# Conditioning work in a two-layer encoder trunk: row blocks requested a step ahead, sums placed later, half of the work moved to the second weight group

## The chip, the cores and the metric

The kernel runs on one core of a Trainium2 chip, as one launch. The metric is the device time of the launch in microseconds. The comparison between kernels is made with unprofiled runs; the views of the trace come from one profiled execution.

The core has a matrix engine (TensorE, in the profile PE, its weight loads PEld), a vector engine (VectorE, DVE), a scalar engine (ScalarE, ACT), GpSimd (POOL) and a queue that issues most of the DMA transfers (SyncE, SP). Each engine carries out its own list of instructions in order and waits on semaphores for the others.

## What is computed

The reference is a trunk of two layers on x of shape (1, 512, 1024) in f32. A layer has three sublayers: a half-step SwiGLU FFN, a mixer (a state-space scan, an attention and a short convolution side by side), and a second half-step FFN. Every sublayer is conditioned on one vector c:

```python
mod = (c_act @ ada_w[l] + ada_b[l]).reshape(b, N_SUB, 3, 1, D_MODEL)   # shift, scale, gate for each sublayer

h = modulate(x, mod[:, 0, 0], mod[:, 0, 1])            # x * (1 + scale) + shift
y = swiglu_ffn(h, ffn1_w_in[l], ffn1_w_out[l])
x = layer_norm(ALPHA * x + 0.5 * mod[:, 0, 2] * y, ln_g[l, 0], ln_b[l, 0])
```

`swiglu_ffn` is `(silu(gate) * up) @ w_out` with `gate, up` the halves of `h @ w_in`; the inner width is 2816. `ada_w` has the shape (2, 1024, 9216), 75 MB in f32, and is read once: c is one row, so each of its 18 column blocks of 1024 is a product of a vector with a 1024x1024 matrix. This part is the one that the change touches.

## The kernel before, in words

**Sublayers.** They are numbered s = 0 to 5; s = 0, 2, 3, 5 are FFNs, s = 1 and 4 are mixers. The activations lie in four token tiles of 128. Every large product is made of three f32r matmuls (`mm3`): both operands are split into a rounded high half and the remaining low half, and high x low, low x high and high x high are added in PSUM. Weights are loaded by SP into raw tiles (`ri` for w_in, `ro` for w_out; two buffers), ScalarE writes their high half (`hi`, `ho`), VectorE the low half (`li`, `lo`).

**An FFN.** `ffn` goes through 11 pairs `jp` of 256 inner columns, the first six as group 0, the other five as group 1. For each pair two column units (gate and up) are loaded and split, then come 96 matmuls into the tiles `pf`, then Silu, the product (`af`) and its split (`ah`, `al`). After each group `out_proj` multiplies what the group made by its rows of w_out (tiles `po`), in two halves of 512 output columns, and folds the result into x with the gate. In the last group's second half the token tiles are finished one after the other: fold, layer-norm statistics, norm; then PE transposes the tile (`ptr`), ScalarE applies scale and shift (`hf`) and rounds (`hh`), VectorE writes the low half (`hl`). The last token tile's transposes come only in the next sublayer, behind its first products (`last_tile`): an FFN's pair 0 takes token columns 0 to 255 first, and in their midst (`POS`) calls `last_tile`; then it takes columns 256 to 511, for which the last `hl` is needed.

**The conditioning work.** `ada_acc` makes one accumulator of 1024 columns: eight row blocks `ra` of 512 KB are requested on SP (L233; two buffers), and VectorE multiplies each by a column of c and adds it to `acc`, in two halves of 512. Then `acc_split` splits the accumulator (`gh` on ScalarE, `gl` on VectorE; `gl` takes one of the two buffers of the row blocks), and a sum over the partitions follows as two matmuls with ones for each half (`acc_sum`): into `pg` for a gate, to which the bias is then added, or into `pm` for a scale or shift, from which VectorE takes the diagonal and reduces it (`dg`, `sums`). `ada_gate(s)` makes the gate of a sublayer, `ada_ss(s)` its scale and shift, two accumulators one after the other.

**Where it stands in the program.** These are generators, and the FFN advances them by ticks: one tick behind the loads of each column unit (two for each pair) and one behind each row unit of `out_proj` (three for each half). A tick adds a number of credits (2.7 for s = 0 and 3, 1.3 for s = 2 and 5), and each yield costs one; a yield of `TICK` ends the tick and leaves the credit that is there. What is left is drained behind token tile 0 of the last half of `out_proj`. The first FFN of a layer makes the gates of s and s+1 and the scales and shifts of s+1 and s+2 (six accumulators), the second FFN the gate of s and the scale and shift of s+1 (three; one for s = 5).

**What sets the order.** The program's order is a priority. A planner that works ahead of time sorts each engine's instructions by it and by when, on its own estimates, an instruction is ready; the result is a fixed list for each engine. `after(ins, prev)` forces an order on one engine: the first accumulation of an accumulator stands behind the last `hl` that was written in the program before it (`ln_done`), and so do the splits of pair 1. Nearly all instructions of TensorE, VectorE and ScalarE go through one helper, so they carry its line, L52; the views tell them apart by tiles.

## Time and profile before

| | us |
|---|---|
| median of 3 runs | 1988.9 |
| the runs | 1988.61 to 1991.4 |
| profiled execution, its own time | 1988.45 |
| span of the trace in it | 1986.7 |
| TensorE busy in the span | 1937.8 (98%) |
| VectorE busy | 1206.4 (61%) |
| ScalarE busy | 705.8 (36%) |

In the lines shown below, a group or a timeline row names the engine, the operation, the tile it writes, `<-`, the tiles it reads, the shapes and a count. A timeline row begins with its start and its length in us, and a bracket tells how long the engine had stood idle before it and what ended that. A row of the waits reads: who waited, for whom, us in total, how often, the longest. Matmuls overlap, so TensorE's busy time is not its time at full rate.

### The profile page before, as it was taken

The numbers are of one execution on the slowest core, as the hardware profiler recorded it, in microseconds if no ns is written. First come the engines' busy times: TensorE is split into PE (matmuls) and PEld (weight loads), VectorE is DVE, ScalarE is ACT, GpSimd is POOL, SyncE is SP. The second block draws the span as 40 slices with busy tenths as digits, with TensorE's granted clock in tenths as the row PEclk, the third lists the DMA queues.
The fourth block names the chain that finished last, engine by engine and source line by source line (L and its number), as shares of the span: only waits on it lengthen the run. The fifth ranks groups of instructions, "written<-read, shape, count | busy, mean of one in ns | idle before, by whom it ended". The sixth has DMA issues, their size and how long they took to land.

```text
span 1986.7 us, 23052 instructions
## 1 busy us (share of the span) xinstructions
PE 1937.8 (98%) x9230; PEld 1616.3 (81%) x9230; DVE 1206.4 (61%) x1804; ACT 705.8 (36%) x1126; POOL 97.8 (5%) x126
## 2 busy tenths in 40 slices
PE   5999999999999999999999999999999999999998
PEld 4787888888878888888888788788888788888887
DVE  8886753477867655643478757436786676333336
ACT  3432222264575332132253222323546643222220
POOL 0100000012100000000000000000140000000000
PEclk9999999999999999999999999999999999999999
DMA  9675542143222544432256656322322243223321
GB/s 329 213 256 193 186 163 96 54 128 106 85 75 82 173 140 167 138 128 83 98 170 201 222 165 227 102 89 65 119 84 96 75 141 129 92 91 121 106 85 43
DMA packets 176730, 263.95 MB, mean 133 GB/s; under 512 B 9806, under 2 KB 124628, under 8 KB 176624
## 3 DMA queue, kind: packets, MB, share of 16 engines
q1 hardware_dynamic: 174000, 254.98, 38.7%
q0 software_dynamic: 2624, 7.52, 1.3%
q8 instruction: 72, 1.18, 0.2%
q14 instruction: 34, 0.28, 0.0%
HBM read 260.37 MB, written 2.10 MB: 132 GB/s over the span
## 4 chain that ended last, share of the span: by engine, by line
PE 81%; DVE 8%; DMA 6%; ACT 3%; issue 1%; POOL 0%; SPq 0%; POOLq 0%; DVEq 0%; ACTq 0%
PE pf L52 39%; PE po L52 26%; DMA ra<-in_ada_w_dram 5%; DVE acc L52 2%; PE pz L52 2%; PE pjm4x L52 1%; PE pjm1x L52 1%; ACT hf L52 1%; DVE li L52 1%; DVE af L52 1%; PE py L52 1%; DVE x L52 1%; PE pfo L52 1%; PE pjm1c L52 1%; PE pjm1k L52 1%
## 5 line engine op out<-in xcount | busy, mean ns | idle before, releaser
L52 PE MATMUL pf<-hl,hi 128*128 128x512 f32 (+1 forms) x1504 | 567.1, 377 | 7.5 <-DVE hl L52 7.5
L52 PE MATMUL pf<-hh,li 128*128 128x512 f32 (+1 forms) x1504 | 567.6, 377 | 1.5 <-DVE li L52 1.2
L52 PE MATMUL pf<-hh,hi 128*128 128x512 f32 (+1 forms) x1504 | 566.4, 377 | 0.0
L52 PEld LDWEIGHTS pf<-hl,hi 128*128 128x128 f32 x1504 | 284.7, 189 | 59.9 <-DVE hl L52 8.8
L52 PEld LDWEIGHTS pf<-hh,li 128*128 128x128 f32 x1504 | 284.7, 189 | 53.0 <-DVE li L52 1.7
L52 PEld LDWEIGHTS pf<-hh,hi 128*128 128x128 f32 x1504 | 284.6, 189 | 50.6
L52 DVE TENSOR_TENSOR li<-ri,hi 128x1024 fp32r<-128x1024 f32 x176 | 214.0, 1221 | 181.6 <-ACT hi L52 181.3
L52 ACT ACTIVATE hi<-ri 128x1024 fp32r<-128x1024 f32 x176 | 185.7, 1060 | 350.4 <-PE pf L52 214.4
L52 PE MATMUL po<-ho,al 128*128 128x512 f32 (+1 forms) x704 | 273.3, 388 | 0.4 <-DVE af L52 0.4
L52 PE MATMUL po<-lo,ah 128*128 128x512 f32 (+1 forms) x704 | 272.9, 388 | 0.0
L52 PE MATMUL po<-ho,ah 128*128 128x512 f32 (+1 forms) x704 | 272.6, 388 | 0.0
L52 DVE TENSOR_TENSOR lo<-ro,ho 128x1024 fp32r<-128x1024 f32 x104 | 127.1, 1223 | 206.8 <-ACT ho L52 206.6
L52 DVE SCALAR_TENSOR_TENSOR acc<-ra,cT,acc 128x512 f32<-128x512 f32 x224 | 157.6, 746 | 76.8 <-DMA ra<-in_ada_w_dram 76.3
L52 ACT ACTIVATE ho<-ro 128x1024 fp32r<-128x1024 f32 x104 | 110.0, 1058 | 257.6 <-PE po L52 156.2
L52 ACT ACTIVATE sg<-pf 128x512 f32<-128x512 f32 x88 | 52.5, 596 | 294.0 <-PE pf L52 293.9
L52 PEld LDWEIGHTS po<-ho,al 128*128 128x128 f32 x704 | 132.2, 188 | 27.9 <-DVE af L52 0.8
L52 PEld LDWEIGHTS po<-lo,ah 128*128 128x128 f32 x704 | 132.2, 188 | 27.0
L52 PEld LDWEIGHTS po<-ho,ah 128*128 128x128 f32 x704 | 132.2, 188 | 26.9
L52 DVE TENSOR_TENSOR af<-sg,pf 128x512 f32<-128x512 f32 x88 | 60.1, 684 | 145.8 <-PE pf L52 145.8
L52 ACT ACTIVATE hf<-ptr,modB,modA 128x128 f32<-128x128 f32 (+1 forms) x168 | 66.9, 489 | 98.1 <-PE ptr L52 84.5
L450 POOL TENSOR_TENSOR rs<-ve,mhalf 128x1 f32<-128x1 f32 x28 | 17.2, 616 | 1354.1 <-DVE ve L52 1352.7
L52 ACT ACTIVATE ah<-af 128x512 fp32r<-128x512 f32 x88 | 54.5, 619 | 29.9 <-DVE af L52 28.8
(407 smaller groups left out, 2361.9 us busy)
## 6 DMA issues: line engine op xcount, KB each, us to landing
ri<-in_ffn_w_in_dram SPq DMA_DIRECT2D x88, 1024.0 KB, 5.0
ra<-in_ada_w_dram SPq DMA_DIRECT2D x128, 512.0 KB, 4.6
ro<-in_ffn_w_out_dram SPq DMA_DIRECT2D x40, 1024.0 KB, 4.9
ro<-in_mix_w_out_dram SPq DMA_DIRECT2D x8, 1024.0 KB, 5.0
rf<-in_ada_w_dram SPq DMA_DIRECT2D x8, 512.0 KB, 7.3
ro<-in_ffn_w_out_dram SPq DMA_DIRECT2D x8, 512.0 KB, 3.6
rf<-in_ada_w_dram SPq DMA_DIRECT2D x16, 192.0 KB, 6.2
gate<-in_ada_b_dram SPq DMA_DIRECT2D x12, 256.0 KB, 5.7
```

The lines of the kernel that those rows point to most:

```text
L52: ins = f(*a, **k)
L450: pool.tensor_tensor(rs, ve, mhalf[:, 0:1], ALU.pow)
```

## The change

- `ada_acc` requests row block k+1 ahead of the accumulation of block k, and has one more yield, behind the request of block 0.
- `ada_ss` and `ada_gate` yield `TICK` twice, not once, between the split and the sum.
- The first FFN of a layer begins with the gate of s and the scale and shift of s+1 alone; the gate of s+1 and the scale and shift of s+2 are added when group 1 begins. The pace of these FFNs is 2.2 credits a tick instead of 2.7.
- In the FFNs s = 2, 3 and 5, pair 0 has no tick behind its loads; each of the two adds half the credits of one, and one tick stands behind `last_tile`.
- A tick that finds nothing pending sets the credit to zero.

```diff
-CR = (2.7, 1.3)
+CR = (2.2, 1.3)
@@ ada_acc
         acc = [slot([P, 512], F32, f"acc{l}_{col}_{h}") for h in range(2)]
+        raws = []
+
+        def row_block(k):
+            raws.append(adap.tile([P, D], F32, tag="ra", name=f"ra{l}_{col}_{k}"))
+            sp.dma_start(raws[k], w[:, k, col:col + D])
+
+        row_block(0)
+        yield acc
         for k in range(KD):
-            raw = adap.tile([P, D], F32, tag="ra", name=f"ra{l}_{col}_{k}")
-            sp.dma_start(raw, w[:, k, col:col + D])
+            if k + 1 < KD:
+                row_block(k + 1)
             for h in range(2):
-                rk = raw[:, h * 512:(h + 1) * 512]
+                rk = raws[k][:, h * 512:(h + 1) * 512]
@@ ada_ss, and the same in ada_gate
             parts = acc_split(acc)
             yield TICK
+            yield TICK
@@ begin, tick
-    def begin(*gens):
+    def begin(pace, *gens):
         pending.extend(gens)
         credit[0] = 0.0
-        credit[1] = len(pending) and CR[0] if len(gens) > 2 else CR[1]
+        credit[1] = pace
     def tick():
         credit[0] += credit[1]
+        if not pending:
+            credit[0] = 0.0
@@ ffn
-    def ffn(s, w_in, w_out):
+    def ffn(s, w_in, w_out, *later):
         for gi, grp in enumerate((range(0, 6), range(6, NPAIR))):
             acts = []
+            if gi == 1:
+                pending.extend(later)
...
-                    tick()
+                    if s == 0 or jp > 0:
+                        tick()
+                    else:
+                        credit[0] += credit[1] / 2
...
                     if jp == 0 and i == POS:
                         last_tile[0](mm_last[0])
+                        tick()
@@ the loop over the sublayers
         if j == 0:
-            begin(ada_gate(s), ada_ss(s + 1), ada_gate(s + 1), ada_ss(s + 2))
-            ffn(s, ffn1_w_in[l], ffn1_w_out[l])
+            begin(CR[0], ada_gate(s), ada_ss(s + 1))
+            ffn(s, ffn1_w_in[l], ffn1_w_out[l], ada_gate(s + 1), ada_ss(s + 2))
...
-            begin(ada_gate(s), *([ada_ss(s + 1)] if s < 5 else []))
+            begin(CR[1], ada_gate(s), *([ada_ss(s + 1)] if s < 5 else []))
```

## The prediction

> **What bounds the kernel now.** I read the page first, then TensorE's waits, then the timeline around each wait, then the vector queue.

> ```profile
> span 1986.7 us, 23052 instructions
> PE 1937.8 (98%) x9230; PEld 1616.3 (81%) x9230; DVE 1206.4 (61%) x1804; ACT 705.8 (36%) x1126; POOL 97.8 (5%) x126
> ra<-in_ada_w_dram SPq DMA_DIRECT2D x128, 512.0 KB, 4.6
> ```

> TensorE is busy for 98%, and the change leaves it the same matmuls. So only its stops can be won or lost. Those that end on something the conditioning work touches:

> ```profile
> PE pf L52 <- DVE hl L52: 7.5, 4, 2.7
> PE pm L52 <- ACT gh L52: 6.2, 4, 2.3
> PE pg L52 <- DVE gl L52: 0.4, 1, 0.4
> PE po L52 <- DVE af L52: 0.4, 1, 0.4
> ```

> The same stops, one by one, on TensorE's timeline:

> ```profile
> 85.10 0.51 PE L52 MATMUL pg<-gl,onesr 128*128 128x512 f32 x1 [0.45 <-DVE gl L52]
> 152.48 0.51 PE L52 MATMUL pm<-gh,onesr 128*128 128x512 f32 x1 [1.26 <-ACT gh L52]
> 266.67 0.50 PE L52 MATMUL pm<-gh,onesr 128*128 128x512 f32 x1 [1.17 <-ACT gh L52]
> 651.80 0.58 PE L52 MATMUL pf<-hl,hi 128*128 128x256 f32 x1 [2.50 <-DVE hl L52]
> 1022.48 0.39 PE L52 MATMUL pf<-hl,hi 128*128 128x256 f32 x1 [2.13 <-DVE hl L52]
> 1126.80 0.50 PE L52 MATMUL pm<-gh,onesr 128*128 128x512 f32 x1 [1.53 <-ACT gh L52]
> 1243.68 0.51 PE L52 MATMUL pm<-gh,onesr 128*128 128x512 f32 x1 [2.26 <-ACT gh L52]
> 1629.11 0.39 PE L52 MATMUL pf<-hl,hi 128*128 128x256 f32 x1 [2.68 <-DVE hl L52]
> ```

> Three stand at the start of an FFN (s=2, 3, 5), five at a sum over partitions. What VectorE did before the first and the third of those three:

> ```profile
> 644.00 0.69 DVE L52 TENSOR_TENSOR hl<-hf,hh 128x512 fp32r<-128x512 f32 x1 [0.89 <-ACT hh L52]
> 649.73 1.42 DVE L52 SCALAR_TENSOR_TENSOR acc<-ra,cT,acc 128x512 f32<-128x512 f32 x2 [5.03 <-DMA ra<-in_ada_w_dram]
> 651.06 0.68 DVE L52 TENSOR_TENSOR hl<-hf,hh 128x512 fp32r<-128x512 f32 x1
> ...
> 1627.04 1.42 DVE L52 SCALAR_TENSOR_TENSOR acc<-ra,cT,acc 128x512 f32<-128x512 f32 x2 [5.21 <-DMA ra<-in_ada_w_dram]
> ```

> And what ScalarE had ready:

> ```profile
> 645.05 0.63 ACT L52 ACTIVATE hh<-hf 128x512 fp32r<-128x512 f32 x1
> ```

> The last token tile's hl could have run at 645.7, when hh was done. It ran at 651.06, because an accumulation in front of it in VectorE's queue waited 5.03 us for a row block. TensorE came to the end of its other work 2.50 us before 651.80, that is at 649.3.

> Two of the three stops cost more than their length (windows of TensorE: length, busy, count, granted clock):

> ```profile
> 651.80:655.20 3.40, 3.40 (x16) 0.50 0.54 161
> 655.20:658.60 3.40, 3.40 (x30) 1.00 1.00 318
> 1023.82:1027.23 3.41, 3.41 (x18) 0.50 0.81 250
> 1027.23:1030.64 3.41, 3.41 (x30) 1.00 0.91 272
> 1626.00:1634.00 8.00, 5.32 (x44) 1.00 0.44 136
> ```

> After the stops at 651.80 and 1022.48 the granted clock is 0.50 for 3.4 us, and 14 and 12 fewer matmuls fit than in the next 3.4 us (0.113 us each): 1.6 + 1.4 = 3.0 us. After the stop at 1629.11 the clock stays at 1.00.

> **None ahead of the last tile.** The first accumulation carries an order edge behind the last hl issued. With the tick moved behind the last tile, that edge names the last tile's hl, so no row block can hold it. hl then ends about 646.5, before 649.3. What is late next: the accumulations, behind which wait the li splits of pair 1's second unit. They have the second half of pair 0 and one product group as cover, more than 10 us (96 half-width matmuls x 0.113). The gate's two bias requests move on SP with the tick; the first who needs them is the gate's sum, pairs later. POOL issues nothing of what moves. Gain: 2.50 + 2.13 + 2.68 = 7.3, and 3.0 of clock.

> **Sums two units behind the split.** The two ticks of one pair follow each other with no matmul between. With one tick between split and sum, both can fall ahead of the same matmuls, and TensorE then stands for the chain of row block, accumulation, gh. With two ticks a whole pair, or a half of the output projection, lies between. Counted through the generators, this holds for every sum. Gain: 1.26 + 1.17 + 1.53 + 2.26 + 0.45 = 6.7. The 0.4 before po goes too: the accumulations that stood ahead of that af belong to gate s+1, which moves to the second group.

> At each of the eight stops TensorE also loses its overlap:

> ```profile
> 1181.59 0.39 PE L52 MATMUL pg<-gh,onesr 128*128 128x512 f32 x1
> 1181.82 0.39 PE L52 MATMUL pg<-gl,onesr 128*128 128x512 f32 x1
> ...
> 1215.17 0.39 PE L52 MATMUL pm<-gh,onesr 128*128 128x512 f32 x1
> ```

> A matmul lasts 0.39 with 0.23 to the next, so a stop hides 0.16 more: 8 x 0.16 = 1.3. **Removed in all: 7.3 + 3.0 + 6.7 + 0.4 + 1.3 = 18.7 us.**

> **Row blocks one step ahead.** This adds no DMA, matmul or vector instruction, only one credit per accumulator (10 for 9). Within a burst it changes nothing, since there are two buffers:

> ```profile
> 1182.71 0.34 SPq L233 DMA_DIRECT2D ra<-in_ada_w_dram  x1
> ...
> 1187.88 7.18 SPq L233 DMA_DIRECT2D ra<-in_ada_w_dram  x3
> ...
> 1197.28 8.30 SPq L233 DMA_DIRECT2D ra<-in_ada_w_dram  x3
> ```

> ```profile
> 1186.98 0.87 DVE L52 TENSOR_SCALAR acc<-ra,cT 128x512 f32<-128x512 f32 x2
> ...
> 1210.14 1.36 DVE L52 TENSOR_TENSOR gl<-acc,gh 128x512 fp32r<-128x512 f32 x2
> ```

> A request goes out when the accumulation two blocks back ends (1187.85, then 1187.88). Moved past weight loads on SP, seven requests can hold them; in this burst the breaks between the three rows are weight loads, and TensorE did not stop behind one. I count 0, with bounds from -1 (waits of VectorE not listed above shrink) to +3.

> **Second half with the second group.** The second group has 16 ticks (two for each of five pairs, six in the projection), 35.2 credits at 2.2 for the 30 of three accumulators; a TICK ends its tick and leaves the credit, which then goes out at once. Followed tick by tick, the last accumulator of s=0 and s=3 runs as a burst of seven blocks in the last output projection, its split in front of the second half, its sum in the drain behind tile 0. Before, nothing of this stood there. The burst above is the model: from the sum at 1181.59 to the end of gl (1211.50) 29.9 us, while TensorE came to the next sum after 33.6.

> VectorE over the same stretch of the last projection (first half and tile 0), and over the rest of the tail:

> ```profile
> 1328.60:1362.80 34.20, 15.84 (x21) 1.00 0.22 62
> 1362.80:1394.00 31.20, 21.85 (x39) 1.00 0.25 77
> ```

> What comes in (groups of the model burst's window, then of the whole run):

> ```profile
> L52 DVE SCALAR_TENSOR_TENSOR acc<-ra,cT,acc 128x512 f32<-128x512 f32 x14 | 9.8, 746 | 6.8 <-DMA ra<-in_ada_w_dram 6.8
> ```

> ```profile
> L52 DVE TENSOR_TENSOR dg<-pm,ident 128x512 f32<-128x512 f32 x20 | 13.2, 684 | 0.0
> L52 DVE TENSOR_REDUCE sums<-dg 128x4 f32<-128x512 f32 x20 | 12.8, 675 | 0.0
> ```

> 15.8 + 16 x 0.746 + 1.4 (gl) + 2 x (0.684 + 0.675) for the sum ahead = 31.9, and 6.8 of waiting: 38.7 in 34.2, 4.5 late. The cover, tile 0:

> ```profile
> 1365.94 0.81 DVE L52 TENSOR_SCALAR x<-x,mv,rs 128x1024 f32<-128x1024 f32 x1 [0.75 <-POOL rs L450]
> ```

> ```profile
> 1369.23 1.04 PE L52 MATMUL ptr<-ident,x 128*128 128x128 f32 x8
> ```

> Its norm ends at 1366.75, 2.5 us before TensorE asks for it. So 2.0 us may show, at two places: 4.0. The drain's own dg and sums (2.7) fit into 31.2 - 21.9 = 9.3 us idle. Bounds: 0 if the waits fall into VectorE's present idle time; above, 4.5 + 2.7 + 1.5 of half clock = 8.7 at each place, 17.4. I take 4.0, nearer the lower end, because the model burst was done 3.7 us early.

> **Sum.** The profiled execution took 1988.45 us (span 1986.7 and 1.75 around it). 1988.45 - 18.7 + 4.0 = 1973.75; the median of the runs lies 0.45 higher: **1974.2 us**.

> **Rivals.**
> (1) The tail keeps the whole 4.5 us and a half-clock window (1.5) at both places: 12.0 for the 4.0, 1982.2. For it: VectorE's demand above; against: the 2.5 us of cover and the lo splits that already wait for buffers.
> (2) The half clock is not caused by the stops: then 3.0 stay, 1977.2. For it: the stop at 1629.11, the longest, brought none; against: both windows begin within 1.4 us of a stop's end.
> (3) Slower: the last accumulators' bursts take one block at a time, because the low half of a split (gl) sits in one of the two row-block buffers. Seven blocks of 4.6 landing and 2 x 0.746 then take 42.6 where the model took 27.4 (1182.71 to 1210.14), 15.2 more: gl is ready 45.1 us after the sum against 33.6 and 34.2 of cover in the two projections. That is 11.5 + 10.9 in each of two FFNs, and four half-clock windows: 44.8 + 6 = 51 for the 4.0, 2021. It decides from about 10 us in all. Against it: the sum frees gl ahead of the burst, as at 1181.59.
> (4) It doesn't do what it says: accumulations still pass the last hl. Then 7.3 + 3.0 + 0.5 stay: 1985.0.

> [...]

> **Numbers.** Forecast 0.63 (own range 1969 to 1980), rival 1 0.17, rival 2 0.08, rival 3 0.07, rival 4 0.05. 0.2% is 4 us, about what a measurement tells from no change, so faster means below 1984.9. Forecast, 1 and 2 are faster, less 0.02 for the upper end of rival 1: 0.86. Rival 4 and that 0.02: same, 0.07. Rival 3: slower, 0.07. Range 1968 to 1986: below, the 1 us bound and no tail cost (1969.2) with a little room; above, rivals 1 and 4.

> **What would show it.** Right: no stop of pf behind hl at the three FFN starts, clock 1.00 there, no stop of pm behind gh; acc still waits for ra, with VectorE alone idle. Wrong: new stops in the last projection of s=0 and s=3 before ptr, pm or po, or the clock at 0.50 there.

## The result and the profile after

| | before | after |
|---|---|---|
| unprofiled runs, median (lowest to highest), us | 1990.15 (1988.61 to 1991.45) | 1971.71 (1969.50 to 1972.77) |
| profiled execution, us | 1988.45 | 1972.77 |
| its span, us | 1986.7 | 1971.1 |

The ratio of after to before is 0.9904, with a 95% interval of 0.9888 to 0.9919: 18 to 19 us less. The forecast was 1974.2 and the range 1968 to 1986.

The page of the changed kernel: span, busy times, the accumulations with the idle time ahead of them, the requests of row blocks.

```profile
span 1971.1 us, 23078 instructions
PE 1934.5 (98%) x9230; PEld 1614.9 (82%) x9230; DVE 1204.2 (61%) x1804; ACT 704.6 (36%) x1126; POOL 98.5 (5%) x126
L52 DVE SCALAR_TENSOR_TENSOR acc<-ra,cT,acc 128x512 f32<-128x512 f32 x224 | 158.2, 748 | 88.9 <-DMA ra<-in_ada_w_dram 87.8
ra<-in_ada_w_dram SPq DMA_DIRECT2D x128, 512.0 KB, 4.8
```

The matmuls are the same 9230. VectorE waits 87.8 us for row blocks (76.3 before), and TensorE does not feel it. Four of the rows of TensorE's waits in the changed kernel (tile and engine that waited, what for: us in all, times, longest):

```profile
PE pmf L52 <- DVE af L52: 15.8, 2, 11.8
PE pm L52 <- DVE gl L52: 1.6, 2, 1.1
PE pf L52 <- DVE li L52: 1.0, 1, 1.0
PE pf L52 <- DVE hl L52: 0.2, 1, 0.2
```

All eight stops that the prediction listed are gone (the 0.2 of `pf` behind `hl` lies at 48.25, in the first FFN). New are two of `pm` behind `gl`. VectorE's timeline at the start of the FFN s=2 (start, duration, instruction, idle time before it):

```profile
643.70 0.69 DVE L52 TENSOR_TENSOR hl<-hf,hh 128x512 fp32r<-128x512 f32 x1 [3.04 <-ACT hh L52]
645.41 0.69 DVE L52 TENSOR_TENSOR hl<-hf,hh 128x512 fp32r<-128x512 f32 x1 [1.02 <-ACT hh L52]
646.02 0.88 DVE L52 TENSOR_SCALAR acc<-ra,cT 128x512 f32<-128x512 f32 x2
646.81 2.35 DVE L52 TENSOR_TENSOR li<-ri,hi 128x1024 fp32r<-128x1024 f32 x2
649.09 1.41 DVE L52 SCALAR_TENSOR_TENSOR acc<-ra,cT,acc 128x512 f32<-128x512 f32 x2
```

The last `hl` runs as soon as ScalarE has `hh`, at 645.41 (651.06 before), and the accumulations come behind it. TensorE over the three FFN starts (window: length, busy time and count of TensorE, TensorE's weight loads, VectorE, ScalarE, GpSimd, then granted clock, DMA share, GB/s):

```profile
646.00:649.40 3.40, 3.40 (x30) 3.40 (x30) 3.40 (x6) 0.68 (x1) 0.00 (x0) 1.00 0.42 96
1010.00:1018.00 8.00, 8.00 (x69) 8.00 (x68) 6.40 (x9) 2.99 (x7) 0.00 (x0) 1.00 0.52 157
1608.00:1616.00 8.00, 8.00 (x69) 8.00 (x68) 6.57 (x10) 4.28 (x8) 0.00 (x0) 1.00 0.48 142
```

TensorE is busy without a break and the clock stays at 1.00. What is left of a cost of the conditioning work lies in the last projection of s=0 and of s=3. First VectorE there at s=0, then TensorE:

```profile
374.69 1.42 DVE L52 SCALAR_TENSOR_TENSOR acc<-ra,cT,acc 128x512 f32<-128x512 f32 x2 [0.37 <-DMA ra<-in_ada_w_dram]
376.02 1.28 DVE L52 SCALAR_TENSOR_TENSOR gy<-po,gate 128x512 f32<-128x512 f32 x2
...
382.01 1.28 DVE L52 BATCH_NORM_STATS2 st<-x 128x6 f32<-128x512 f32 x2
383.21 1.27 DVE L52 TENSOR_TENSOR gl<-acc,gh 128x512 fp32r<-128x512 f32 x2
```

```profile
383.93 0.50 PE L52 MATMUL pm<-gl,onesr 128*128 128x512 f32 x1 [1.11 <-DVE gl L52]
```

The last accumulation ends at 376.1. Then come the folds and statistics of the projection's first half, 7.2 us of them, and only then `gl`. The row blocks were in time; the split stood at the wrong place of VectorE's list. The stop is 1.11 us here and 0.44 at s=3.

### The profile page after: what moved, and what is told of

Its sections match the earlier page's. It is cut to its first block, busy times and chain, and to the rows that moved or that the text cites. A ratio compares the mean times of both kernels' runs of the same rounds, so it can differ in the third digit from the quotient of the medians.

```text
span 1971.1 us, 23078 instructions
## 1 busy us (share of the span) xinstructions
PE 1934.5 (98%) x9230; PEld 1614.9 (82%) x9230; DVE 1204.2 (61%) x1804; ACT 704.6 (36%) x1126; POOL 98.5 (5%) x126
## 4 chain that ended last, share of the span: by engine, by line
PE 91%; DVE 4%; DMA 2%; ACT 2%; issue 0%; POOL 0%; POOLq 0%; SPq 0%; DVEq 0%; ACTq 0%
PE pf L52 49%; PE po L52 26%; PE pz L52 2%; DMA ra<-in_ada_w_dram 1%; PE pjm4x L52 1%; PE pjm1x L52 1%; PE ptr L52 1%; PE py L52 1%; PE pfo L52 1%; DVE af L52 1%; PE pS L52 1%; DVE acc L52 1%; PE pjm1c L52 1%; PE pjm4c L52 1%; PE pjm1k L52 1%; PE pjm4k L52 1%
## 5 line engine op out<-in xcount | busy, mean ns | idle before, releaser
L52 PE MATMUL pf<-hh,li 128*128 128x512 f32 (+1 forms) x1504 | 567.1, 377 | 1.3 <-DVE li L52 1.0
L52 PE MATMUL pf<-hl,hi 128*128 128x512 f32 (+1 forms) x1504 | 565.8, 376 | 0.2 <-DVE hl L52 0.2
L52 PE MATMUL pf<-hh,hi 128*128 128x512 f32 (+1 forms) x1504 | 565.5, 376 | 0.0
L52 DVE TENSOR_TENSOR li<-ri,hi 128x1024 fp32r<-128x1024 f32 x176 | 214.6, 1222 | 191.9 <-ACT hi L52 191.7
L52 PEld LDWEIGHTS pf<-hh,li 128*128 128x128 f32 x1504 | 283.7, 189 | 53.5 <-DVE li L52 1.7
L52 PEld LDWEIGHTS pf<-hl,hi 128*128 128x128 f32 x1504 | 283.7, 189 | 51.5 <-DVE hl L52 0.9
L52 PEld LDWEIGHTS pf<-hh,hi 128*128 128x128 f32 x1504 | 283.6, 189 | 51.3
L52 ACT ACTIVATE hi<-ri 128x1024 fp32r<-128x1024 f32 x176 | 185.8, 1059 | 358.5 <-PE pf L52 220.3
L52 PE MATMUL po<-ho,al 128*128 128x512 f32 (+1 forms) x704 | 273.4, 388 | 0.0
L52 PE MATMUL po<-lo,ah 128*128 128x512 f32 (+1 forms) x704 | 272.9, 388 | 0.0
L52 PE MATMUL po<-ho,ah 128*128 128x512 f32 (+1 forms) x704 | 272.7, 388 | 0.0
L52 DVE TENSOR_TENSOR lo<-ro,ho 128x1024 fp32r<-128x1024 f32 x104 | 127.0, 1222 | 158.3 <-ACT ho L52 158.1
L52 DVE SCALAR_TENSOR_TENSOR acc<-ra,cT,acc 128x512 f32<-128x512 f32 x224 | 158.2, 748 | 88.9 <-DMA ra<-in_ada_w_dram 87.8
L52 ACT ACTIVATE ho<-ro 128x1024 fp32r<-128x1024 f32 x104 | 110.0, 1058 | 265.2 <-PE po L52 157.3
L52 DVE TENSOR_TENSOR af<-sg,pf 128x512 f32<-128x512 f32 x88 | 60.2, 685 | 155.4 <-PE pf L52 155.2
L52 ACT ACTIVATE sg<-pf 128x512 f32<-128x512 f32 x88 | 52.6, 597 | 287.1 <-PE pf L52 287.1
L52 PEld LDWEIGHTS po<-ho,ah 128*128 128x128 f32 x704 | 132.2, 188 | 27.2
L52 PEld LDWEIGHTS po<-lo,ah 128*128 128x128 f32 x704 | 132.2, 188 | 26.9
L52 PEld LDWEIGHTS po<-ho,al 128*128 128x128 f32 x704 | 132.2, 188 | 26.7
L52 ACT ACTIVATE hf<-ptr,modB,modA 128x128 f32<-128x128 f32 (+1 forms) x168 | 67.1, 492 | 101.8 <-PE ptr L52 86.8
L52 ACT ACTIVATE ah<-af 128x512 fp32r<-128x512 f32 x88 | 54.5, 620 | 23.0 <-DVE af L52 22.9
## 6 DMA issues: line engine op xcount, KB each, us to landing
ra<-in_ada_w_dram SPq DMA_DIRECT2D x128, 512.0 KB, 4.8
rf<-in_ada_w_dram SPq DMA_DIRECT2D x8, 512.0 KB, 7.6
ro<-in_ffn_w_out_dram SPq DMA_DIRECT2D x8, 512.0 KB, 3.6
```

The source lines that it names most:

```text
L52: ins = f(*a, **k)
```

## The experiments

Theory A, the prediction's: the gain comes from two edits, the last tile's tick (10.3 with its half clock) and the second TICK (8), and the request ahead is worth nothing. Rivals: the request ahead or the new pace and grouping carry part of it, or the half clock has another cause. Each run leaves one edit out, does one alone, or changes one size; the ratios below are to the kernel before.

**The last tile's part alone.** The kernel before, with this:

```diff
-                    tick()
+                    if s == 0 or jp > 0:
+                        tick()
+                    else:
+                        credit[0] += credit[1] / 2
...
                         last_tile[0](mm_last[0])
+                        tick()
```

> The kernel before with one part of the change alone: in the FFNs s = 2, 3 and 5 the ticks of pair 0 move behind the last token tile. Theory (the accumulations in front of the last hl make the three stops, and the stops bring the half clock): the stops of pf behind hl and both half-clock windows go, the five stops at the sums stay: 7.3 + 3.0 + 0.5 = 10.8 us less than the kernel before. Rival A (the half clock has another cause): 7.8 less. Rival B (the wait only moves on, to the weight splits of pair 1 behind the accumulations): less than 2 us gained, with new stops of pf behind li.

1979.46 us, ratio 0.9944 (0.9926 to 0.9962), that is 11 us less (7.6 to 14.7). Three of the rows of TensorE's waits in it:

```profile
PE pm L52 <- ACT gh L52: 5.8, 4, 1.9
PE pg L52 <- DVE gl L52: 0.4, 1, 0.4
PE pf L52 <- DVE hl L52: 0.2, 1, 0.2
```

`pf` behind `hl` went from 7.5 to 0.2 and the half clock behind it is gone (span 1976.2, 10.5 below before, where the stops alone are 7.3 and their overlap 0.5); the stops at sums stayed. This part is shown, with its size.

**The grouping and the pace alone.** The kernel before, with these edits of the change (and those of `begin` and of a tick that finds nothing pending):

```diff
-CR = (2.7, 1.3)
+CR = (2.2, 1.3)
...
-    def ffn(s, w_in, w_out):
+    def ffn(s, w_in, w_out, *later):
...
+            if gi == 1:
+                pending.extend(later)
...
-            begin(ada_gate(s), ada_ss(s + 1), ada_gate(s + 1), ada_ss(s + 2))
-            ffn(s, ffn1_w_in[l], ffn1_w_out[l])
+            begin(CR[0], ada_gate(s), ada_ss(s + 1))
+            ffn(s, ffn1_w_in[l], ffn1_w_out[l], ada_gate(s + 1), ada_ss(s + 2))
```

> The kernel before with the second half of the work moved to the second group and the pace of 2.2 alone; one tick between split and sum, requests in step, ticks in pair 0 as before. The three stops at the FFN starts stay in every theory. Theory 1 (a sum stops TensorE where no unit of matmuls lies between its split and itself): that holds for the last accumulator of each group, four in all, 1.7 us each, for 8.3 us at five before: about 1 us less than the kernel before. Theory 2 (what decides is TensorE's time from one sum to the next, against the 29.9 us that a burst of blocks and its split took): the last sum of the first group comes one pair (22.7 us) behind the one before it and stops TensorE 7.2 us and brings a half clock (1.5); the last of the second group comes 28 us behind and stops it 2: two of each are 21 for the 8.3, some 13 us slower than before.

1989.34 us, ratio 0.9992 (0.9982 to 1.0003): no gain. The stops moved but did not go (its trace is of the longest of its ten executions, 1994.60). One of the new places:

```profile
380.75 1.02 PE L52 MATMUL pm<-gh,onesr 128*128 128x512 f32 x2 [1.53 <-ACT gh L52]
385.36 0.50 PE L52 MATMUL pm<-gl,onesr 128*128 128x512 f32 x1 [1.10 <-DVE gl L52]
```

**One TICK in place of two.** The changed kernel, in `ada_ss` and `ada_gate`:

```diff
             parts = acc_split(acc)
             yield TICK
-            yield TICK
```

> The changed kernel with one tick instead of two between split and sum. In the two first FFNs of a layer three sums then have no matmul between their split and themselves (the scale of s+1, the scale of s+2 and the shift of s+2); from sum to sum TensorE has two pairs (43.6 us) ahead of the first two and a half of the projection (28 us) ahead of the third. Theory 1 (unit between split and sum): three stops of 1.7 us in each, 10 us for the 1.6 of the changed kernel, 8 to 9 slower than it. Theory 2 (time from sum to sum against 29.9 us): only the third stops, 2 to 3 us in each, 3 to 5 slower than the changed kernel.

1987.18 us, ratio 0.9980 (0.9967 to 0.9993): 15 us above the changed kernel, more than either theory had. TensorE's timeline, and what VectorE did ahead of the third of these stops:

```profile
377.33 1.02 PE L52 MATMUL pm<-gh,onesr 128*128 128x512 f32 x2 [1.53 <-ACT gh L52]
383.44 0.56 PE L52 MATMUL pm<-gl,onesr 128*128 128x512 f32 x1 [2.55 <-DVE gl L52]
808.26 1.02 PE L52 MATMUL pm<-gh,onesr 128*128 128x512 f32 x2 [1.67 <-ACT gh L52]
1351.45 1.02 PE L52 MATMUL pm<-gh,onesr 128*128 128x512 f32 x2 [1.53 <-ACT gh L52]
```

```profile
758.29 1.42 DVE L52 SCALAR_TENSOR_TENSOR acc<-ra,cT,acc 128x512 f32<-128x512 f32 x2 [1.07 <-DMA ra<-in_ada_w_dram]
...
809.48 1.29 DVE L52 TENSOR_TENSOR gl<-acc,gh 128x512 fp32r<-128x512 f32 x2
```

At 808.26 the accumulator had been complete since 759.7, 48 us earlier, and its split still ran only just ahead of the sum: where the split is written right before the sum, it also runs there. That is what the second TICK cures: in the changed kernel this sum starts at 833.83, and its split was complete 28 us earlier. With one TICK the waits at `pm` and `po` are 8.2 us against 1.6, and there are two half-clock windows where the changed kernel has none behind a stop (0.50 from 383.74 to 387.15; matmuls 0.43 apart, not 0.23, from 1353.32 to 1355.88; some 3 us at the 1.5 for one that the prediction counted): 9.6 of the 12.2 us between the two spans. Where the other 2.6 went was not found.

**A quicker pace.** The changed kernel, second TICK kept:

```diff
-CR = (2.2, 1.3)
+CR = (3.3, 1.3)
```

> The changed kernel with a pace of 3.3 credits instead of 2.2 in the first FFN of a layer, so that all eight blocks of an accumulator go out in one tick. Two ticks still lie between split and sum. Theory 1: the scales of s+1 and s+2 keep a pair between split and sum and don't stop; only the last sum (split and sum both ahead of the first half of the last projection) does, 1.7 us: within 2 us of the changed kernel. Theory 2: these scales' sums come one pair, 22.7 us, behind the sum before, and so does the last: three stops of about 7 us in each of two FFNs, with half clock (1.5): up to 50 us slower than the changed kernel.

1997.80 us, ratio 1.0037 (1.0019 to 1.0055): slower than before. One of its four long stops on TensorE, and VectorE ahead of it:

```profile
130.30 1.46 PE L52 MATMUL pm<-gh,onesr 128*128 128x512 f32 x2 [5.35 <-ACT gh L52]
```

```profile
105.05 0.88 DVE L52 TENSOR_SCALAR acc<-ra,cT 128x512 f32<-128x512 f32 x2
...
115.86 1.42 DVE L52 SCALAR_TENSOR_TENSOR acc<-ra,cT,acc 128x512 f32<-128x512 f32 x2 [3.52 <-DMA ra<-in_ada_w_dram]
...
127.51 2.74 DVE L52 SCALAR_TENSOR_TENSOR acc<-ra,cT,acc 128x512 f32<-128x512 f32 x4 [4.03 <-DMA ra<-in_ada_w_dram]
130.55 1.29 DVE L52 TENSOR_TENSOR gl<-acc,gh 128x512 fp32r<-128x512 f32 x2
```

With two ticks a unit does lie between split and sum, and TensorE stops all the same. The reason shows when the sums are set side by side. For sums whose accumulator runs as one burst behind the sum before it (times from the starts of the sums on TensorE, the last `gl` on VectorE):

| kernel, sum | from the sum before, us | `gl` complete after that sum, us | stop, us |
|---|---|---|---|
| before, 1126.8 | 26.2 | 27.9 | 1.5 |
| before, 1243.7 | 28.5 | 30.2 | 2.3 |
| pace 3.3, 130.3 | 28.5 | 30.0 | 5.4 |
| pace 3.3, 336.3 | 26.8 | 29.1 | 4.0 |
| before, 1215.2 | 33.6 | 29.9 | 0 |
| after, 203.9 | 33.6 | 27.7 | 0 |
| after, 1168.8 | 33.6 | 27.5 | 0 |
| after, 382.4 | 32.8 | 34.9 | 1.1 |
| one TICK, 203.9 | 53.2 | 31.5 | 0 |

A burst of eight row blocks and its split take 27 to 32 us from the sum before. The first column holds the stop too, so a sum that comes after less than that stops. Fourteen more sums, here and in the runs above, came 25 to 30 us behind the one before and stopped too, for 1.0 to 4.4 us; four of the fourteen, in the last projections, also had `gl` behind the folds. Two did not stop: at pace 3.3, in the last projections, sums came 29.6 and 28.5 us behind the one before, with `gl` complete after 31.3 and 30.2. One of them on TensorE:

```profile
364.46 0.50 PE L52 MATMUL po<-ho,al 128*128 128x512 f32 x1 [0.61 <-DVE af L52]
...
365.84 0.50 PE L52 MATMUL pm<-gh,onesr 128*128 128x512 f32 x1
366.18 0.39 PE L52 MATMUL po<-ho,ah 128*128 128x512 f32 x1
```

Here TensorE's list has the sum's four matmuls among those of the projection, which cover the wait; the accumulations cost it 0.61 and 0.35 us another way, for an `af` that stood behind them in VectorE's list. The last line of the table has a single tick and does not stop. So two things count: TensorE's work between two sums, which the pace sets too and not the second TICK alone, and where the split stands in VectorE's list. The row at 382.4 is the second case (the folds ahead of `gl`).

**No split over the groups.** The changed kernel, all six accumulators pending from the start at pace 2.2:

```diff
-            begin(CR[0], ada_gate(s), ada_ss(s + 1))
-            ffn(s, ffn1_w_in[l], ffn1_w_out[l], ada_gate(s + 1), ada_ss(s + 2))
+            begin(CR[0], ada_gate(s), ada_ss(s + 1), ada_gate(s + 1), ada_ss(s + 2))
+            ffn(s, ffn1_w_in[l], ffn1_w_out[l])
```

> The changed kernel with all six accumulators pending from the start of a layer's first FFN, not the last three from the second group on; the pace stays 2.2. The last sum then stands at the start of the last projection, two pairs behind the sum before, and no burst and no sum stand in the last projection. Theory (the tail is the only place where the change added a stop): the two stops of pm behind gl go, 1.6 us less than the changed kernel, no new stop. Rival (the slots: 24 of 28 hold the first group's products, and the gate and the accumulator of s+1 want four more): the products or the accumulator wait for slots, and TensorE stops at the first group's projection, some us more than the changed kernel.

1968.77 us, ratio 0.9891 (0.9874 to 0.9908): 2.9 below the changed kernel's median, with no stop at any sum: the last one comes at 350.1, early in the last projection, 46.9 us behind the sum before, and no burst and no split of it are left for that projection's end.

**The drain one tile later.** The changed kernel, with

```diff
-                    if t == 0:
+                    if t == 1:
                         drain()
```

> The changed kernel with the drain behind token tile 1 of the last projection instead of tile 0, so that the last sum has 6.8 us more of matmuls ahead of it. Theory (in the tail gl is late because it stands behind the first half's folds in the vector queue): the two stops of pm behind gl (1.11 and 0.44 us) go and nothing else changes: 1.6 to 2 us less than the changed kernel. Rival (the vector engine has no time left in the tail): the stop reappears at a transpose or at the first products of the mixer, and the time stays.

1968.89 us, ratio 0.9891 (0.9874 to 0.9908). VectorE's list is as before, with `gl` behind the folds, but the sum comes 5 us later (TensorE's timeline):

```profile
387.52 0.39 PE L52 MATMUL pm<-gh,onesr 128*128 128x512 f32 x1
387.75 0.39 PE L52 MATMUL pm<-gl,onesr 128*128 128x512 f32 x1
```

Both runs take away the tail's two stops (1.55 us in all) by different means and save 2.8 to 2.9 by their medians; the ratios' intervals overlap with the changed kernel's, and the clock at the kernel's start alone makes some 1.5 us from one execution to the next (below), so the size is not settled beyond that.

**No request ahead.** The changed kernel, each block requested in its own step, the extra yield kept:

```diff
-        row_block(0)
...
-            if k + 1 < KD:
-                row_block(k + 1)
+            row_block(k)
```

> The changed kernel with each row block requested in the step of its own accumulation, as before; the additional yield stays, so all sums stand where they stand in the changed kernel. Theory (two buffers set when a request can go out, not its place in the program): the same time within 1 us, and the same waits of acc for ra within some us. Rival (the request ahead is what took the waits away): the vector engine waits longer for ra, and the stops at the sums come back, up to 8 us slower than the changed kernel.

1970.70 us, ratio 0.9903 (0.9886 to 0.9919): the same as the changed kernel. VectorE's wait ahead of the accumulations, 87.8 us there:

```profile
L52 DVE SCALAR_TENSOR_TENSOR acc<-ra,cT,acc 128x512 f32<-128x512 f32 x224 | 158.1, 747 | 88.3 <-DMA ra<-in_ada_w_dram 88.0
```

The edit that stands first in the change's title is worth nothing here. The queue's list shows why: from 303 to 386 us its requests stand in the same order in both kernels, with the same weight loads between, 1.9 to 2.9 us apart, as the sums at both ends of this stretch are by 1.9. With two buffers a request goes out when a buffer comes free, in either place in the program: before, at 1187.88, when the accumulation two blocks back had ended at 1187.85; in the changed kernel at 370.88, when it had ended at 370.86.

**Both left out.** The last two edits together (no split over the groups, no request ahead), so that beside the pace and the added yield the last tile's tick and the second TICK remain.

```diff
-        row_block(0)
...
-            if k + 1 < KD:
-                row_block(k + 1)
+            row_block(k)
...
-            begin(CR[0], ada_gate(s), ada_ss(s + 1))
-            ffn(s, ffn1_w_in[l], ffn1_w_out[l], ada_gate(s + 1), ada_ss(s + 2))
+            begin(CR[0], ada_gate(s), ada_ss(s + 1), ada_gate(s + 1), ada_ss(s + 2))
+            ffn(s, ffn1_w_in[l], ffn1_w_out[l])
```

> The changed kernel with the split over groups and the row-block request one step ahead both left out: all six accumulators are pending from the FFN's start at pace 2.2, each block is requested in its own step; the sums two units behind the split and the last tile's tick behind its output pass stay. Theory 1 (sums and last tile carry the whole gain; request ahead is worth nothing, as its own run showed): within 2 us of the run without the split over groups (1968.8), some 3 us under the changed kernel, and no stop of TensorE at a sum over partitions. Theory 2 (with six accumulators queued one behind the other the ring of two blocks is fuller, and the request ahead covers it): 4 us or more above that run, with stops of 1 us and more at scale sums.

1969.12 us, ratio 0.9880 (0.9858 to 0.9902), and no stop at a sum. The whole gain, with less code.

**A late hl on purpose.** The changed kernel, with a chain of 9, 12 and 16 vector multiplications ahead of the last `hl` of s=2, 3 and 5; they write a tile that nothing reads.

```diff
+    LATE = {2: 9, 3: 12, 5: 16}
...
+            wait = ln_done[0]
+            for _ in range(LATE.get(s, 0) if (t, q) == (NT - 1, 1) else 0):
+                d = dve.tensor_tensor(late, late, late, ALU.mult)
+                after(d, wait)
+                wait = d
...
+            after(ln_done[0], wait)
```

> The changed kernel with a chain of 9, 12 and 16 additional vector multiplications of 512 columns (0.68 us each, on a tile that nothing else uses) put ahead of the last token tile's last hl in the FFNs s = 2, 3 and 5, so that TensorE stops there for about 2.2, 4.3 and 7 us. Theory (a stop of TensorE is what halves the granted clock, and a stop of over 3.4 us always does): half clock directly behind the stops of 4.3 and 7 us, each 3.4 us long or a little more and costing 1.5 us; behind the stop of 2.2 us by chance of its place. Rival (the half clock has another cause): no half clock within the run. In time: 2.2 + 4.3 + 7 = 13.5 us more than the changed kernel, and 3 to 5 us more with the half clock.

The stops came out shorter than expected, 0.31, 0.33 and 2.88 us (1976.12 us, one run): the chain of nine, for one, began at 642.45 already, before `hh` was done at 643.51. The longest of them (TensorE's timeline), and the clock behind it (windows):

```profile
1619.95 0.39 PE L52 MATMUL pf<-hl,hi 128*128 128x256 f32 x1 [2.88 <-DVE hl L52]
```

```profile
1618.12:1621.53 3.41, 1.58 (x13) 1.58 (x14) 3.38 (x6) 0.00 (x0) 0.00 (x0) 1.00 0.00 0
1621.53:1624.95 3.42, 3.42 (x19) 3.42 (x18) 2.76 (x4) 2.60 (x3) 0.00 (x0) 0.50 0.70 194
```

A stop of less than 3 us, made on purpose, is followed by half clock, and the two short ones are not (1.00 from 649.50 to 653.00 behind the first; matmuls 0.12 apart ahead of the second and behind it). The same with longer chains:

```diff
-    LATE = {2: 9, 3: 12, 5: 16}
+    LATE = {2: 13, 3: 18, 5: 23}
```

> As the run with vector multiplications ahead of the last hl at s=2, 3 and 5, with longer chains (13, 18 and 23 of 0.72 us in place of 9, 12 and 16); they write a tile that nothing reads. Theory 1 (a stop inside one step of the clock record's 3.41 us grid is enough for a half clock in the next step, as after the stops of 2.50 and 2.13 before): stops of about 3, 4.5 and 7.5 us at the three FFN starts, all three followed by half clock of 3.4 us or more; 1971.1 + 15 + about 5 = some 1991 us of span. [...]

Stops of 0.69, 4.33 and 7.97 us; the first without a half clock (1.00 from 652.60 to 656.00), the others followed by it (1988.23 us, one run; span 1986.2, 15.1 above the changed kernel's; the three stops are 13.0 of it, the half clocks some 3). The second of them:

```profile
1024.10:1027.51 3.41, 3.41 (x18) 3.41 (x18) 3.41 (x6) 1.08 (x2) 0.00 (x0) 0.50 0.51 145
1027.51:1030.92 3.41, 3.41 (x29) 3.41 (x29) 3.09 (x4) 2.02 (x3) 0.00 (x0) 1.00 0.71 232
```

The half clock behind the 7.97 us (0.50 from 1631.67 to 1635.08, 1.00 from there to 1638.50) lasts no longer than that behind the 2.88: one such window of TensorE's work. At pace 3.3 it lasts longer: behind the stop of 5.35 us the clock is at half from 129.87 to 136.69, almost two windows of work. All six stops of over 3.4 us in these traces behind a kernel's first 60 us, the 4.33 and 7.97 here and 5.35, 3.98, 4.22 and 4.40 at pace 3.3, were followed by half clock. The first stop missed its length, so this run alone does not tell a short stop from a long one; the run before it does.

## Why the prediction was right, and where it was off

**None ahead of the last tile: right, in size too.** Counted 7.3 + 3.0 and 0.5 at an output projection; alone it gave 11 (7.6 to 14.7). Its steps are in the trace: `hl` directly behind `hh`, no stop, clock 1.00.

**The sums: the amount right, the reason incomplete.** Counted 6.7 + 1.3 = 8.0; between the last tile's part alone (0.9944) and the whole change (0.9904) lie 0.4%, 8.0 us; that is net of the 1.55 of tail stops, so some 9.5 without them, and each of the two ratios is known to some 3.5 us, so the 1.5 above the count says nothing. But "with two ticks a whole pair, or a half of the output projection, lies between" is not what decides. At pace 3.3 it lies between and TensorE stops for 4 to 5 us; with one TICK nothing lies between, and sums 53 us apart do not stop (one 77 us apart does, its split standing right ahead of it). The step that failed is the reason itself, that a unit of matmuls between split and sum is enough for every sum: what has to be counted is TensorE's time from the sum before against the 27 to 32 us of the burst, and the pace of 2.2 with the second TICK brings it to 32.8 and more at every sum. Pace and grouping alone brought nothing, the second TICK alone was not tried.

**The row blocks: right.** Counted 0 with bounds of -1 to +3; left out, the time stays within about 1 us of the changed kernel's.

**The tail: the place right, size and mechanism off.** Counted 4.0 for two places; the trace shows 1.11 + 0.44 = 1.55, and without them the kernel is some 2.9 faster by the medians. The step that failed is the sum of VectorE's demand (38.7 in 34.2 us): the burst was complete at 376.1, before the sum at 382.4, so the demand fitted. What was late was `gl`, put behind eight fold instructions and four statistics in VectorE's list, which a sum of durations over the stretch can't show. (The burst had eight row blocks, where the prediction's words have seven; its sum counts eight.) Rival 1 (4.5 at both places and half clock) is out. So is rival 3: the burst did not go block by block.

**Rival 2 is out** (the half clock not caused by stops): it went with the stops in the run of the last tile's part alone, and came back with a stop made on purpose. **Rival 4 is out**, by the eight stops that are gone.

**What the balance lacked.** 1988.45 - 18.7 + 1.55 = 1971.3; the profiled execution took 1972.77. The rest stands at the kernel's start. TensorE's timeline there, of after:

```profile
33.91 0.63 PE L52 MATMUL pf<-hh,li 128*128 128x512 f32 x1
34.33 0.63 PE L52 MATMUL pf<-hl,hi 128*128 128x512 f32 x1
...
35.91 0.39 PE L52 MATMUL pf<-hh,hi 128*128 128x512 f32 x1
```

of before:

```profile
33.74 0.39 PE L52 MATMUL pf<-hl,hi 128*128 128x512 f32 x1
33.97 0.40 PE L52 MATMUL pf<-hh,hi 128*128 128x512 f32 x1
```

The matmuls of after are 0.42 apart up to 35.7, those of before 0.23 already at 33.7. Over 30.8 to 37.6 us after has 21 matmuls where before has 30: nine at 0.2 are under 2 us, about the 1.5 that the balance lacks. By the record of the clock the full rate comes at 35.7 us in after and at 30.5 in before; with the request ahead left out it comes at 31.0, with the drain moved (an edit that leaves the kernel's start as it is) at 31.8, without the split over the groups at 35.3. So it goes with the execution, not with an edit. Its price shows at the first output projection: TensorE begins it at 170.8 to 171.2 us in after, without the split, with both left out and with one TICK (full rate at 35.3 to 36.0), and at 169.3 to 169.5 in the four other kernels made from the changed one at pace 2.2 (30.8 to 31.8). So two medians of a few executions can lie some 1.5 us apart by this alone.

## What to carry to other kernels

When an engine that is busy for 98% stops at a product of another engine, measure from one such point to the next: the time that the producer's burst takes against the time that the busy engine needs to come there, and look at where the last piece of the burst stands in the producer's list. Moving one small step behind what the busy engine waits for next was worth 11 us here, requesting data earlier into a full ring nothing. A short stop costs more than its length when a half clock follows (1.6 and 1.4 us more behind the stops of 2.50 and 2.13 before).

## What was not expected of the hardware

| TensorE still within a step, us | steps | followed by half clock |
|---|---|---|
| 0.6 to 1.34 | 45 | 0 |
| 1.34 to 1.65 | 12 | 4 |
| 1.8 to 3.41 | 13 | 13 |

(One more step, with 0.44, was itself at half clock, behind a step of full rest, and was followed by another; so was one of the four in the middle row, with 1.62.) So 1.8 us of rest in a step, some half of it, were enough each time here, and a stop that a boundary of the grid cuts in two can pass without cost. That fits the stop of 2.68 at 1629.11 before, which the boundary at 1627.98 cuts into 1.55 and 1.13 and which brought none, and that of 2.13 at 1022.48, 2.07 of it in one step, which did. What separates the steps between 1.34 and 1.65 that brought a half clock from those that did not stays open.
